# Moving three output groups into the attention's fill, and a final stage that goes token by token

## The chip, the core and the metric

The kernel runs on one core of one Trainium2 chip. The metric is the device time of one launch in microseconds (us). A core has five engines that run their own instruction queues side by side: TensorE (PE; its weight loads are listed as PEld), VectorE (DVE), ScalarE (ACT), GpSimd (POOL) and SyncE (SP). In this kernel SP issues every DMA, in the order of its queue; an issue that waits holds up all that stand behind it.

## The reference

The input is one sequence of 2048 tokens with 1024 values each. One layer is computed: an RMS norm, one input projection to six parts (`q`, `k`, `v`, an attention gate, the input of a recurrence, its gate), two groups of heads, one output projection, an RMS norm and a residual.

```python
h = rmsnorm(x, pre_norm_g)
q, k, v, g_attn, x_lru, g_lru = split(h @ w_in)
o = diff_attention(q, k, v, lam)          # 8 heads, causal, two softmaxes per head, value width 128
y_attn = rmsnorm(o, subln_g) * (1 - lam_init) * silu(g_attn)
y_lru = rg_lru(conv(x_lru)) * silu(g_lru)
y = concatenate([y_attn, y_lru]) @ w_out  # 2048 -> 1024
x = x + rmsnorm(y, post_norm_g)
```

The last norm needs all 1024 outputs of a token, and each output needs all heads. So a token's output can't be finished before the last head's attention on that token is.

## The kernel before, in words

Products of 32-bit values are made of three matmuls: each operand is split into a high part and the rest, and high x high, rest x high and high x rest are added in PSUM. A block of 128 tokens by 512 outputs over 1024 inputs takes 8 x 3 = 24 matmuls of 512 columns; I call it a group.

The program runs in stages: the input projection of the first half of the sequence with the recurrence; attention for tokens 0 to 1023 (with the other half's projection as fill); the second half's recurrence; attention for tokens 1024 to 2047, which matters here; and a final stage.

**The second attention** (`attention`, called with pairs 4 to 7) goes through 8 heads. A pair is 256 tokens, and a head has four pairs of four units (two blocks of 128 tokens, two softmaxes): 128 units, and 12 steps that drain the pipeline. A unit's scores (`s`, L642) are made one step ahead, DVE takes the maximum, ACT the exponentials; some steps later the weights are transposed on PE (`pw`, L715), split by ACT and DVE (`wh`, `wl`, L719 and L720), and multiplied with the values (`o`, L738). Every two pairs of a head (512 tokens, called `j`; `j` = 2 is tokens 1024 to 1535, `j` = 3 the rest) are normalised in six steps: sums over partitions by PE (`pm`, L760), a reciprocal root by DVE (`f`), which goes out to DRAM as `r_s` (L773) and comes back spread over partitions as `rb` (L777), POOL's product `yt` (L782), and the store into `ya_s[j]` (L785). A head's keys come by `ks<-k_s` (L600); the third key block of a head takes the buffer of a block that the head before uses up to its last unit, so it can't be loaded much ahead.

**Fill.** In every step the loop also takes matmuls of the output projection from the generator `fill_out`: 8.25 a step (`FB`). Its groups go through four sets of weights, (rows of `w_out`, half of the outputs): recurrence left and right (16 groups each), attention left and right for the token blocks 0 to 7 (8 each), whose attention part was done in the first half, and one more: attention right for block 8. Sums so far lie in DRAM (`part_s`). In the last set the group is complete on its right, so `finish` (L963) runs the token block's ending: two squares on ACT, two products on POOL, a chain of small DVE operations, an addition to `x`, a store. All groups use one PSUM buffer (`f`), so a group begins when the one before has been read out (L1058). When the set changes, `load_wo` loads eight new blocks of weights through two buffers (`woraw`, L950), each split by POOL. Block `i`'s input is loaded by `load_y` (L958) and split by POOL in quarters (L70, L71).

**Final stage.** Blocks 9 to 15 lack both attention halves, block 8 its left one. The pool `y` holds this stage's tiles. First `load_ya` for blocks 9 and 10; then three right halves (`right`, blocks 9, 10 and 11) with the right weights that are still there, while the eight blocks of left weights come (`woraw`, L1123, two buffers; DVE splits both parts, L203 and L204). Then for each block 8 to 15 its left half and ending (`left`), and after blocks 8 to 11 the right half of the block four further on. `right` loads the partial sums (L1108). The matmuls are `ps_y`, L1098.

The framework keeps each engine's queue in one order that it works out when the program is built, and it makes every wait. What stands in a queue is not always in the order of the source.

Of the kernel before, what the change touches and what calls it, by code (L numbers as in the profile page):

```python
# [18 lines left out]
P = 128  # L19
S = 2048  # L20
D = 1024
# [22 lines left out]
def hymba_kernel(  # L44
# [544 lines left out]

    def attention(prs, kv_p, e_p, a_p, ps_s, ps_w, ps_o, nsb, fill, per_slot, kbufs, vbufs, p1bufs):
        NS = len(prs)
        nmax = (prs[-1] + 1) * 256
# [188 lines left out]

        def norm6(h, j):
            nc.sync.dma_start(out=ya_s[j][:, h, :], in_=nrm.pop((h, j))[1])  # L785

        units = [(h, pr, t, c) for h in range(H) for pr in prs for t in range(2) for c in range(2)]
        U = len(units)
# [43 lines left out]
        for s in range(U + 12):  # L832
            ops = todo.get(s, [])

            def run(kind, fn):
                for k, a in ops:
                    if k == kind:
                        fn(*a)

            for k, fn in (("K", load_k), ("VV", load_v), ("Q", load_q), ("G", load_g)):  # L840
                run(k, fn)
            u = units[s] if s < U else None
            nx = units[s + 1] if s + 1 < U else None
            na = len(pieces(u)[1]) if u else 0
            npc = len(pieces(nx)[1]) if nx else 0
            if u:
                score_exp(u)
            tp = 0.15 + SP / 1200.0
            free = [0.0 if k < nsb - na else tp * (k - nsb + 1 + na) + 0.1 for k in range(npc)]
            ts = [a for k, a in ops if k == "T"]  # L850
            vs = [a + (e,) for k, a in ops if k == "V" for e in range(2)]
            owed += per_slot(s)
            nf = int(owed)
            clock, k = 0.0, 0
            while k < npc or ts or vs or nf > 0:
                if k < npc and (free[k] <= clock or not (vs or ts or nf > 0)):
                    score_mm(nx, k)
                    score_max(nx, k)
                    clock = max(clock, free[k]) + 0.43 * SP / CH
                    k += 1  # L860
                elif ts and clock >= T_AT:
                    transpose_w(*ts.pop(0))
                    clock += 0.43
                elif nf > 0:
                    r = next(fill, "end")
                    if r == "end":
                        nf = 0
                    elif r == "group":
                        owed -= 1
                        nf = 0 if k < npc or s < U else nf  # L870
                    else:
                        nf -= 1
                        owed -= 1
                    clock += 0.216
                elif vs and not ts:
                    values(*vs.pop(0))
                    clock += 0.33
                elif ts:
                    transpose_w(*ts.pop(0))
                    clock += 0.43  # L880
            run("C", combine)
            run("N1", norm1)
            run("N2", norm2)
            run("N3", norm3)
            run("N4", norm4)
            run("N5", norm5)
            run("N6", norm6)
# [123 lines left out]
    with ExitStack() as pb:  # L1011
# [4 lines left out]
        ps_w = pb.enter_context(tc.tile_pool(name="ps_wB", bufs=2, space=PSUM))  # L1016
        ps_o = pb.enter_context(tc.tile_pool(name="ps_oB", bufs=1, space=PSUM))
        ps_f = pb.enter_context(tc.tile_pool(name="ps_fB", bufs=1, space=PSUM))
        groups = [(r, nh, i) for r, nh in wsets for i in range((8, 16)[r])] + [(0, 1, 8)]

        def fill_out():
            ysp, parts = load_y(*groups[0][::2])
# [1 line left out]
                split(*p)  # L1024
            nc.sync.dma_start(out=pgt, in_=post_norm_g[0].partition_broadcast(P))
            for g, (r, nh, i) in enumerate(groups):
                ps = ps_f.tile([P, CH], F32, tag="f", name="f")
                yh, yl = ysp
                nxt = groups[g + 1] if g + 1 < len(groups) else None
                if nxt:  # L1030
                    ysp, parts = load_y(*nxt[::2])
                part = None
                c0 = nh * CH
                if i >= 8 and r == 0:
                    yv = f_p.tile([P, D], F32, tag="yv", name="yv", bufs=1)
                    nc.sync.dma_start(out=yv, in_=part_s[1][i])
                    part = yv[:, CH:]
                    ys[i], yvs[i] = ysp, yv
                elif r == 0:
                    if nh:  # L1040
                        yv = f_p.tile([P, D], F32, tag="yv", name="yv", bufs=1)
                        nc.sync.dma_start(out=yv[:, 0:CH], in_=part_s[0][i][:, 0:CH])
                    part = f_p.tile([P, CH], F32, tag="part", name="part", bufs=1)
                    nc.sync.dma_start(out=part, in_=part_s[1][i][:, c0:c0 + CH])
                for k in range(8):
                    hi, lo = wo[r, nh, k]
                    for m, (a, b) in enumerate(((yh, hi), (yl, hi), (yh, lo))):
                        nc.tensor.matmul(  # L1048
                            out=ps, lhsT=a[:, k, :], rhs=b, start=(k == 0 and m == 0), stop=(k == 7 and m == 2),
                        )  # L1050
                        if (k, m) != (7, 2):
                            yield
                    if nxt and nxt[:2] != (r, nh):
                        load_wo(*nxt[:2], k)
                    if k % 2 and nxt:
                        split(*parts[k // 2])
                if r == 0 and nh == 1:
                    nc.vector.tensor_tensor(out=yv[:, CH:], in0=ps, in1=part, op=ALU.add)  # L1058
                    ends[i] = finish(f_p, i, yv, 1, 1, nc.gpsimd if i < FE else nc.vector)
                    if i < 8:  # L1060
                        ends.pop(i)()
                else:
                    st = f_p.tile([P, CH], F32, tag="fo", name="fo", bufs=1)
                    if part:
                        nc.vector.tensor_tensor(out=st, in0=ps, in1=part, op=ALU.add)
                        nc.sync.dma_start(out=part_s[0][i][:, 0:CH], in_=st)
                    else:
                        nc.scalar.activation(out=st, in_=ps, func=AF.Copy)
                        nc.sync.dma_start(out=part_s[1][i][:, c0:c0 + CH], in_=st)
                yield "group"  # L1070

        attention(
            range(4, 8), kvB_p, e_p, a_p, ps_s, ps_w, ps_o, 4 * CH // SP, fill_out(),
            lambda s: FB if s > 1 else 6, 6, 5, 1,
        )

    with ExitStack() as p3:  # L1080
        y_p = p3.enter_context(tc.tile_pool(name="y", bufs=2))
        ps_y = p3.enter_context(tc.tile_pool(name="ps_y", bufs=6, space=PSUM))

        def load_ya(i):
            raw = y_p.tile([P, 8, P], F32, tag="yraw3", name="yraw3")
            nc.sync.dma_start(out=raw, in_=ya_s[i // 4][:, :, (i % 4) * P:(i % 4 + 1) * P])
            yh = y_p.tile([P, 8, P], F32R, tag="yh3", name="yh3", bufs=6)
            yl = y_p.tile([P, 8, P], F32R, tag="yl3", name="yl3", bufs=6)
            split3(yh, yl, raw, SY)
            ys[i] = (yh, yl)  # L1090

# [11 lines left out]
        w1 = [wo[0, 1, k] for k in range(8)]  # L1103
        w0 = []

        def right(i):
            yvs[i] = y_p.tile([P, D], F32, tag="yv3", name="yv3", bufs=5)
            nc.sync.dma_start(out=yvs[i], in_=part_s[1][i])  # L1108
            ps = out_mm(i, w1)
            nc.vector.tensor_tensor(out=yvs[i][:, CH:], in0=ps, in1=yvs[i][:, CH:], op=ALU.add)  # L1110
            ends[i] = finish(y_p, i, yvs[i], 2, 1 + (i == 15), nc.vector if FY else nc.gpsimd)

        def left(i):
            ps = out_mm(i, w0)
            nc.vector.tensor_tensor(out=yvs[i][:, 0:CH], in0=ps, in1=yvs[i][:, 0:CH], op=ALU.add)
            ends.pop(i)()

        load_ya(9)
        load_ya(10)
        for i in range(9, 12):  # L1120
            for k in ((0, 1, 2), (3, 4, 5), (6, 7))[i - 9]:
                raw = y_p.tile([P, CH], F32, tag="woraw3", name="woraw3")
                nc.sync.dma_start(out=raw, in_=w_out2[k * P:(k + 1) * P, 0:CH])  # L1123
                hi = y_p.tile([P, CH], F32R, name=f"w3h{k}", bufs=1)
                lo = y_p.tile([P, CH], F32R, name=f"w3l{k}", bufs=1)
                split3(hi, lo, raw, SW)
                w0.append((hi, lo))
            right(i)
            load_ya(i + 2)
        for i in range(8, 16):  # L1130
            left(i)
            if i < 12:
                right(i + 4)
                if i + 6 < 16:
                    load_ya(i + 6)
    pf.close()


# [29 lines left out]
```

## Time and profile before

| | |
|---|---|
| median of 3 runs | 2303.52 us (2302.61 to 2305.75) |
| the profiled execution | 2302.22 us |
| its span, first to last instruction | 2300.4 us |
| PE busy | 2183.5 us (95%) |
| DVE, ACT, POOL busy | 64%, 43%, 35% |
| mean granted clock of PE | 0.980 |

A row of the profile names a line of the code, an engine, an operation and its tiles (what it writes, an arrow, what it reads; the numbers of buffers left out). In rows in order of time the first number is the start, counted from the span's start, and the second the length. Matmuls overlap in the pipeline, so a length of 0.39 us does not mean that the next one starts 0.39 later. An entry on SP is the issue of a DMA; its landing is later.

### The profile page before, as it was taken

The page shows a single profiled execution, that of the slowest core. Times are in us where ns is not written, and L with a number is a line of the kernel's source. Part 1 is how long each engine was busy: PE and PEld are TensorE (multiplying, and loading weights), DVE is VectorE, ACT ScalarE, POOL GpSimd, SP SyncE. Part 2 cuts the span into 40 slices and gives each one's busy share as a digit, 9 for nine tenths or more (in the row PEclk, how much of TensorE's full clock was granted, in tenths as well). Part 3 has the DMA queues.
Part 4 walks back from the last instruction along what each step waited for, and adds up shares of the span by engine and source line. Part 5 has one row for each costly group of instructions (what it writes and reads, how often), then busy time and mean ns, then how long its engine had stood idle before and what let it go on. Part 6 is the DMA issues. An engine that isn't in the chain of part 4 may idle for free. (4 is left out here: it accounts for less than half of the span.)

```text
span 2300.4 us, 31837 instructions
## 1 busy us (share of the span) xinstructions
PE 2183.5 (95%) x11281; PEld 1800.9 (78%) x11281; DVE 1482.6 (64%) x2976; ACT 984.2 (43%) x2227; POOL 804.7 (35%) x773
## 2 busy tenths in 40 slices
PE   7999999999899999999989998999999998999778
PEld 6888888888678878888878775888788886887666
DVE  6532145456576666666237786888888887888565
ACT  4311134434443444444125564665555655555211
POOL 1222034444311111111266553233533335345452
PEclk9999999999999999999999998999999999999989
DMA  6554322332569876864452117456466475655473
GB/s 201 155 150 149 112 86 85 105 106 69 141 155 188 169 172 175 183 165 116 128 179 67 60 37 185 105 138 169 112 156 165 111 147 135 173 138 142 113 258 128
DMA packets 358785, 317.94 MB, mean 138 GB/s; under 512 B 32546, under 2 KB 290659, under 8 KB 358627
## 3 DMA queue, kind: packets, MB, share of 16 engines
q1 hardware_dynamic: 358626, 315.91, 52.8%
q8 instruction: 89, 1.46, 0.3%
q14 instruction: 70, 0.57, 0.1%
HBM read 221.41 MB, written 94.44 MB: 137 GB/s over the span
## 5 line engine op out<-in xcount | busy, mean ns | idle before, releaser
L228 PE MATMUL ps<-hh,whi 128*128 128x512 f32 (+1 forms) x1456 | 569.6, 391 | 2.7 <-DVE hilo L245 2.0
L228 PE MATMUL ps<-hh,wlo 128*128 128x512 f32 (+1 forms) x1456 | 567.4, 390 | 0.0
L228 PE MATMUL ps<-hl,whi 128*128 128x512 f32 (+1 forms) x1456 | 565.2, 388 | 1.1 <-DVE hl L446 1.1
L683 ACT ACTIVATE p<-s,nm 128x512 f32<-128x512 f32 (+3 forms) x640 | 392.1, 623 | 328.7 <-DVE nm L667 220.4
L665 DVE TENSOR_REDUCE mx<-s 128x1 f32<-128x512 f32 (+3 forms) x576 | 341.0, 617 | 114.9 <-PE s L642 96.3
L642 PE MATMUL s<-ks,qs 128*128 128x512 f32 (+2 forms) x1280 | 369.7, 387 | 28.9 <-DMA ks<-k_s 16.8
L200 POOL TENSOR_TENSOR wlo<-wraw,whi 128x1024 fp32r<-128x1024 f32 x88 | 222.7, 2531 | 437.3 <-DVE whi L199 133.3
L228 PEld LDWEIGHTS ps<-hh,whi 128*128 128x128 f32 x1456 | 277.6, 191 | 53.6 <-DVE hilo L245 2.4
L228 PEld LDWEIGHTS ps<-hl,whi 128*128 128x128 f32 x1456 | 277.2, 190 | 52.7 <-DVE hl L446 1.4
L228 PEld LDWEIGHTS ps<-hh,wlo 128*128 128x128 f32 x1456 | 276.6, 190 | 51.1
L642 PEld LDWEIGHTS s<-ks,qs 128*128 128x128 f32 x1280 | 216.4, 192 | 82.3 <-ACT p L683 33.0
L719 ACT ACTIVATE wh<-pw 128x512 fp32r<-128x512 f32 (+1 forms) x288 | 160.3, 577 | 186.5 <-PE pw L715 183.0
L738 PE MATMUL o<-wh,vs 128*128 128x256 f32 (+1 forms) x1152 | 222.5, 283 | 0.0
L720 DVE TENSOR_TENSOR wl<-pw,wh 128x512 fp32r<-128x512 f32 (+1 forms) x288 | 185.4, 653 | 35.8 <-ACT wh L719 34.3
L738 PEld LDWEIGHTS o<-wh,vs 128*128 128x128 f32 x1152 | 193.2, 191 | 18.1 <-ACT wh L719 2.1
L70 POOL TENSOR_SCALAR yh<-yraw 128x256 fp32r<-128x256 f32 x196 | 92.3, 488 | 290.6 <-PE f L1048 267.9
L1048 PE MATMUL f<-woh,yh 128*128 128x512 f32 x392 | 163.2, 416 | 25.0 <-DVE yv L1058 17.9
L782 POOL TENSOR_TENSOR yt<-yt,rb 128x512 f32<-128x512 f32 x32 | 44.1, 1379 | 405.4 <-DMA rb<-r_s 218.7
L701 DVE SCALAR_TENSOR_TENSOR p<-p,rr,p 128x128 f32<-128x128 f32 (+15 forms) x128 | 179.2, 1400 | 2.8
L715 PE MATMUL pw<-ident,p 128*128 128x128 f32 x1088 | 169.4, 274 | 5.8 <-DVE wl L720 4.5
L738 PE MATMUL o<-wl,vs 128*128 128x256 f32 x576 | 163.7, 284 | 8.9 <-DVE wl L720 8.9
L1048 PE MATMUL f<-wol,yh 128*128 128x512 f32 x392 | 163.3, 417 | 0.9 <-POOL wol L71 0.9
(166 smaller groups left out, 3298.7 us busy)
## 6 DMA issues: line engine op xcount, KB each, us to landing
wraw<-in_w_in_dram SPq DMA_DIRECT2D x96, 512.0 KB, 4.8
qs<-q_s SPq DMA_DIRECT2D x128, 256.0 KB, 5.2
vs<-v_s SPq DMA_DIRECT2D x48, 512.0 KB, 6.2
ks<-k_s SPq DMA_DIRECT2D x96, 256.0 KB, 5.5
xt<-in_x_dram SPq DMA_DIRECT2D x32, 512.0 KB, 4.7
k_s<-hilo SPq DMA_DIRECT2D x64, 256.0 KB, 4.2
q_s<-hilo SPq DMA_DIRECT2D x64, 256.0 KB, 3.5
v_s<-hilo SPq DMA_DIRECT2D x32, 512.0 KB, 3.7
```

Source lines behind the costliest of these rows:

```text
L70: nc.gpsimd.tensor_scalar(out=hi, in0=src, scalar1=1.0, scalar2=1.0, op0=ALU.mult, op1=ALU.mult)
L200: nc.gpsimd.tensor_tensor(out=lo, in0=src, in1=hi.bitcast(F32), op=ALU.subtract)
L228: nc.tensor.matmul(out=ps[:, t0:t0 + n], lhsT=a[:, k, :], rhs=b[:, k, t0:t0 + n], start=(k == 0 and m == 0), stop=(k == KC - 1 and m == 2),)
L642: nc.tensor.matmul(out=ps[:, b0 - c0:b0 - c0 + nk], lhsT=qq[:, c, t * P:(t + 1) * P], rhs=kst[h, b0 // CH][:, c, 0:nk], start=(m == 0), st ...
L665: nc.vector.tensor_reduce(out=mx[:, pi:pi + 1], in_=sc[u, pi][:, 0:c1 - c0], axis=AX.X, op=ALU.max)
L683: nc.scalar.activation(out=p[:, c0:c1], in_=sc.pop((u, pi))[:, 0:c1 - c0], func=AF.Exp, bias=negm[u], accum_out=acc,)
L701: nc.vector.scalar_tensor_tensor(out=p0[:, 0:n], in0=p1[:, 0:n], scalar=rr[:, 1:2], in1=p0[:, 0:n], op0=ALU.mult, op1=ALU.add,)
L715: nc.tensor.transpose(pw[:, i * P:(i + 1) * P], wts[h, pr, t][:, kb * P:(kb + 1) * P], ident)
L719: nc.scalar.activation(out=wh[:, 0:n], in_=pw[:, 0:n], func=AF.Copy)
L720: nc.vector.tensor_tensor(out=wl[:, 0:n], in0=pw[:, 0:n], in1=wh[:, 0:n].bitcast(F32), op=ALU.subtract,)
L738: nc.tensor.matmul(out=po[h, j][:, oo:oo + w1 - w0], lhsT=a[:, kb % 4, :], rhs=w[:, w0:w1], start=(kb == 0 and m == 0), stop=(kb == 2 * pr ...
L1048: nc.tensor.matmul(out=ps, lhsT=a[:, k, :], rhs=b, start=(k == 0 and m == 0), stop=(k == 7 and m == 2),)
```

## The change

Token blocks are counted 0 to 15. The change does these things:

- The fill's list ends with attention right for blocks 8, 9, 10 and 11, where it had block 8 alone. These four no longer keep their result on the chip: they are added to the partial sums in DRAM (`part_s[1]`, right half) as the left half of blocks 0 to 7 is. The `finish` of block 8 is no longer begun in the fill.
- The fill says "wait" (and the loop leaves it alone for that step) until the last head's store into `ya_s[2]` has been put into the program (`ya_done`). Block 8's input is loaded only then.
- The rate is 9 matmuls a step where it was 8.25. Before, the fill's list ended in the rest behind the loop.
- The final stage loads all eight blocks of left weights first, with ACT making the high part and DVE the rest, then goes through blocks 8 to 15: a left half each, and ahead of it the right half for 12 to 15. Partial sums are loaded two blocks ahead (`begin`). Input of block 8 is loaded again.
- The pool `y` is on the other side of the memory (where attention's pools were), with 5 and 4 buffers in place of 6 and 5.

```diff
+    ya_done = set()
...
         def norm6(h, j):
             nc.sync.dma_start(out=ya_s[j][:, h, :], in_=nrm.pop((h, j))[1])
+            ya_done.add((h, j))
...
+                    elif r == "wait":
+                        nf = 0
...
-        groups = [(r, nh, i) for r, nh in wsets for i in range((8, 16)[r])] + [(0, 1, 8)]
+        groups = [(r, nh, i) for r, nh in wsets for i in range((8, 16)[r])] + [(0, 1, i) for i in range(8, 12)]
...
             for g, (r, nh, i) in enumerate(groups):
+                if ysp is None:
+                    while (H - 1, i // 4) not in ya_done:
+                        yield "wait"
+                    ysp, parts = load_y(r, i)
+                    for p in parts:
+                        split(*p)
...
-                if nxt:
+                ysp, parts = None, ()
+                if nxt and (nxt[0] or nxt[2] < 8 or (H - 1, nxt[2] // 4) in ya_done):
                     ysp, parts = load_y(*nxt[::2])
...
-                if r == 0 and nh == 1:
+                if r == 0 and nh == 1 and i < 8:
                     nc.vector.tensor_tensor(out=yv[:, CH:], in0=ps, in1=part, op=ALU.add)
-                    ends[i] = finish(f_p, i, yv, 1, 1, nc.gpsimd if i < FE else nc.vector)
-                    if i < 8:
-                        ends.pop(i)()
+                    finish(f_p, i, yv, 1, 1, nc.gpsimd)()
...
-                        nc.sync.dma_start(out=part_s[0][i][:, 0:CH], in_=st)
+                        nc.sync.dma_start(
+                            out=part_s[1][i][:, CH:] if i >= 8 else part_s[0][i][:, 0:CH], in_=st,
+                        )
...
-            lambda s: FB if s > 1 else 6, 6, 5, 1,
+            lambda s: 9 if s > 1 else 6, 6, 5, 1,
...
-        y_p = p3.enter_context(tc.tile_pool(name="y", bufs=2))
+        y_p = p3.enter_context(tc.tile_pool(name="y", bufs=2, side="right"))
...
+        def load_w0(k):
+            raw = y_p.tile([P, CH], F32, tag="woraw3", name="woraw3")
+            nc.sync.dma_start(out=raw, in_=w_out2[k * P:(k + 1) * P, 0:CH])
+            hi = y_p.tile([P, CH], F32R, name=f"w3h{k}", bufs=1)
+            lo = y_p.tile([P, CH], F32R, name=f"w3l{k}", bufs=1)
+            nc.scalar.activation(out=hi, in_=raw, func=AF.Copy)
+            nc.vector.tensor_tensor(out=lo, in0=raw, in1=hi.bitcast(F32), op=ALU.subtract)
+            w0.append((hi, lo))
...
-        for i in range(9, 12):
-            for k in ((0, 1, 2), (3, 4, 5), (6, 7))[i - 9]:
...
-            right(i)
-            load_ya(i + 2)
+        for k in range(8):
+            load_w0(k)
+            if k in (3, 6):
+                load_ya(8 + (k > 3))
+        begin(8)
+        begin(9)
         for i in range(8, 16):
+            if i + 2 < 16:
+                load_ya(i + 2)
+                begin(i + 2)
+            if i >= 12:
+                right(i)
             left(i)
-            if i < 12:
-                right(i + 4)
-                if i + 6 < 16:
-                    load_ya(i + 6)
```

What it moves, as the built programs' queues have it. First SP's queue ahead of the load of head 6's third key block (`ks_18181` before, `ks_18335` after); `woraw` are blocks of `w_out`, `part_s` the partial sums. Before:

```order
L950 DMA woraw_18444<-in_w_out_dram 128x512
L950 DMA woraw_18475<-in_w_out_dram 128x512
L950 DMA woraw_18486<-in_w_out_dram 128x512
L950 DMA woraw_18533<-in_w_out_dram 128x512
L950 DMA woraw_20026<-in_w_out_dram 128x512
L1069 DMA part_s1_15_227<-fo_18541 128x512
L950 DMA woraw_20035<-in_w_out_dram 128x512
L623 DMA gt_18729<-g_s6_2_158 128x512
L600 DMA ks_18181<-k_s6_2_118 64x1024 x2
```

After:

```order
L618 DMA qs_18531<-q_s6_2_86 64x4x256 x2
L1071 DMA part_s0_1_205<-fo_18484 128x512
L1051 DMA part_18545<-part_s1_2_214 128x512
L963 DMA yraw_18929<-ya_s1_197 128x8x128
L1071 DMA part_s0_2_206<-fo_18667 128x512
L1051 DMA part_18691<-part_s1_3_215 128x512
L602 DMA ks_18335<-k_s6_2_118 64x1024 x2
```

The reloads of `w_out` came directly ahead of the keys; now they come 14 rows or more earlier, and a partial-sum store stands there.

Second, SP's queue at the end of attention, from the last head's `r_s` for `j` = 3 on (`ya_s_199` is `ya_s[3]`, `ya_s_198` is `ya_s[2]`). Before:

```order
L773 DMA r_s_3_195<-f_21374 128x4x1
L777 DMA rb<-r_s_3_195 128x512
L986 DMA out_dram<-xt 128x1024
L1042 DMA yv<-part_s_6_210 128x512
L1044 DMA part<-part_s_7_219 128x512
L785 DMA ya_s_199<-yt 128x512
L977 DMA xt<-in_x_dram 128x1024
L1086 DMA yraw_21548<-ya_s_198 128x8x128
L1086 DMA yraw_21554<-ya_s_198 128x8x128
L986 DMA out_dram<-xt 128x1024
L1042 DMA yv<-part_s_7_211 128x512
L1123 DMA woraw_21560<-in_w_out_dram 128x512
```

After:

```order
L775 DMA r_s_3_195<-f_21587 128x4x1
L779 DMA rb<-r_s_3_195 128x512
L1071 DMA part_s_10_222<-fo 128x512
L1051 DMA part<-part_s_11_223 128x512
L787 DMA ya_s_199<-yt 128x512
L1115 DMA woraw_21672<-in_w_out_dram 128x512
L1071 DMA part_s_11_223<-fo 128x512
L1115 DMA woraw_21678<-in_w_out_dram 128x512
L1093 DMA yraw_21696<-ya_s_198 128x8x128
L1115 DMA woraw_21684<-in_w_out_dram 128x512
L1093 DMA yraw_21720<-ya_s_198 128x8x128
L1115 DMA woraw_21690<-in_w_out_dram 128x512
```

In both the final stage's loads stand behind that store; now the left weights are the first of them.

Third, PE's queue where the final stage begins (`f` is the fill, `ps_y` the final stage, `woh`/`wol` the right weights already there, `w3h`/`w3l` the left ones). Before:

```order
L1048 MATMUL f<-woh_20205,yl 128x512
L1048 MATMUL f<-wol_20206,yh 128x512
L1098 MATMUL ps_y<-woh_20028,yh_21550 128x512
L1098 MATMUL ps_y<-woh_20028,yl_21551 128x512
L1098 MATMUL ps_y<-wol_20029,yh_21550 128x512
```

After:

```order
L1055 MATMUL f<-woh_19666,yl 128x512
L1055 MATMUL f<-wol_19667,yh 128x512
L1105 MATMUL ps_y<-w3h_21674,yh_21698 128x512
L1105 MATMUL ps_y<-w3h_21674,yl_21699 128x512
L1105 MATMUL ps_y<-w3l_21675,yh_21698 128x512
```

Three right halves with weights at hand stood first; now the first matmul needs a left block.

More of the change, by code (lines that the diff above doesn't have):

```diff
@@ L1033, in fill_out @@
                 c0 = nh * CH
[L1034 to L1040, printed above, removed]
+                if r == 0:
+                    if nh and i < 8:
                         yv = f_p.tile([P, D], F32, tag="yv", name="yv", bufs=1)
@@ L1054, in fill_out @@
                         load_wo(*nxt[:2], k)
-                    if k % 2 and nxt:
+                    if k % 2 and parts:
                         split(*parts[k // 2])
-                if r == 0 and nh == 1:
+                if r == 0 and nh == 1 and i < 8:
                     nc.vector.tensor_tensor(out=yv[:, CH:], in0=ps, in1=part, op=ALU.add)
-                    ends[i] = finish(f_p, i, yv, 1, 1, nc.gpsimd if i < FE else nc.vector)
-                    if i < 8:
-                        ends.pop(i)()
+                    finish(f_p, i, yv, 1, 1, nc.gpsimd)()
                 else:
@@ L1086, in load_ya @@
             nc.sync.dma_start(out=raw, in_=ya_s[i // 4][:, :, (i % 4) * P:(i % 4 + 1) * P])
-            yh = y_p.tile([P, 8, P], F32R, tag="yh3", name="yh3", bufs=6)
-            yl = y_p.tile([P, 8, P], F32R, tag="yl3", name="yl3", bufs=6)
+            yh = y_p.tile([P, 8, P], F32R, tag="yh3", name="yh3", bufs=5)
+            yl = y_p.tile([P, 8, P], F32R, tag="yl3", name="yl3", bufs=5)
             split3(yh, yl, raw, SY)
@@ L1104, in hymba_kernel, with begin @@
         w0 = []
+        def load_w0(k):
[6 more added lines that the diff above has]
+            w0.append((hi, lo))
+        def begin(i):
+            yvs[i] = y_p.tile([P, D], F32, tag="yv3", name="yv3", bufs=4)
+            nc.sync.dma_start(out=yvs[i], in_=part_s[1][i])
         def right(i):
-            yvs[i] = y_p.tile([P, D], F32, tag="yv3", name="yv3", bufs=5)
-            nc.sync.dma_start(out=yvs[i], in_=part_s[1][i])
             ps = out_mm(i, w1)
             nc.vector.tensor_tensor(out=yvs[i][:, CH:], in0=ps, in1=yvs[i][:, CH:], op=ALU.add)
-            ends[i] = finish(y_p, i, yvs[i], 2, 1 + (i == 15), nc.vector if FY else nc.gpsimd)
         def left(i):
+            ends[i] = finish(y_p, i, yvs[i], 2, 1 + (i == 15), nc.gpsimd)
             ps = out_mm(i, w0)
@@ L1116, in left @@
             ends.pop(i)()
-        load_ya(9)
-        load_ya(10)
-        for i in range(9, 12):
-            for k in ((0, 1, 2), (3, 4, 5), (6, 7))[i - 9]:
[L1122 to L1127, printed above, removed]
-            right(i)
-            load_ya(i + 2)
-        for i in range(8, 16):
+        for k in range(8):
[4 more added lines that the diff above has]
+        begin(9)
+        for i in range(8, 16):
+            if i + 2 < 16:
[3 more added lines that the diff above has]
+                right(i)
             left(i)
-            if i < 12:
-                right(i + 4)
-                if i + 6 < 16:
-                    load_ya(i + 6)
     pf.close()
```

## The prediction

> **What bounds the kernel now.** I read the page first, then busy time by stretch, then TensorE (PE) in order of time around its waits, then the DMA queue of SyncE (SP) around the same places.
>
> ```profile
> span 2300.4 us, 31837 instructions
> PE 2183.5 (95%) x11281; PEld 1800.9 (78%) x11281; DVE 1482.6 (64%) x2976; ACT 984.2 (43%) x2227; POOL 804.7 (35%) x773
> ```
>
> PE is busy for 95% of the span and the change leaves its matmuls as they are, so only PE's idle time (some 117 us) can be won or lost. By stretch (length, then busy time of PE, PEld, DVE, ACT, POOL):
>
> ```profile
> 1480.00:1573.00 93.00, 90.65 (x545) 75.62 (x544) 76.85 (x167) 56.32 (x152) 31.00 (x45) 1.00 0.62 134
> 2033.00:2124.40 91.40, 86.08 (x489) 70.08 (x490) 78.01 (x171) 50.65 (x142) 49.97 (x64) 0.98 0.55 147
> 2124.40:2165.70 41.30, 33.02 (x192) 28.07 (x190) 26.22 (x62) 11.74 (x28) 14.85 (x21) 0.92 0.53 116
> 2165.70:2203.00 37.30, 21.61 (x81) 17.04 (x82) 22.56 (x44) 4.34 (x12) 23.18 (x25) 0.77 0.59 188
> ```
>
> An ordinary head (first row) leaves 2.4 us idle in 93; the two stretches at the end of attention lose 8.3 and 15.7. Here is PE at the waits (start, length, and in brackets the idle time before it and what ended it):
>
> ```profile
> 1566.44 0.47 PE L642 MATMUL s<-ks,qs 128*128 128x256 f32 x2 [1.51 <-DMA ks<-k_s]
> 1940.45 0.77 PE L642 MATMUL s<-ks,qs 128*128 128x256 f32 x2 [10.04 <-DMA ks<-k_s]
> 2124.43 0.72 PE L760 MATMUL pm<-ones,sq 128*128 128x2 f32 x6
> 2165.66 1.05 PE L760 MATMUL pm<-ones,sq 128*128 128x2 f32 x8
> 2167.72 0.47 PE L1048 MATMUL f<-woh,yh 128*128 128x512 f32 x1 [1.00 <-DVE f L766]
> 2195.42 0.77 PE L1048 MATMUL f<-woh,yh 128*128 128x512 f32 x1 [12.20 <-DVE yv L1058]
> 2195.99 0.63 PE L1048 MATMUL f<-woh,yl 128*128 128x512 f32 x1
> 2196.42 0.63 PE L1048 MATMUL f<-wol,yh 128*128 128x512 f32 x1
> 2291.30 0.40 PE L1098 MATMUL ps_y<-w3h,yl 128*128 128x512 f32 x1
> 2291.53 0.40 PE L1098 MATMUL ps_y<-w3l,yh 128*128 128x512 f32 x1
> ```
>
> A warm 512-column matmul takes 0.23 us (last two rows); after a long wait they come every 0.43, and nine did so after 2195.42, which is 1.8 us more. The two `pm` rows are my marks: M1 (2124.43) begins the normalisation of head 7's rows 1024 to 1535, M2 (2165.66) that of its rows 1536 to 2047. PE's last matmul ends at 2291.93, 167.5 us after M1; the final 8.4 us are the last token's ending, which the change leaves alone. And SP's queue:
>
> ```profile
> 1916.35 14.76 SPq L950 DMA_DIRECT2D woraw<-in_w_out_dram  x6
> 1934.12 1.11 SPq L600 DMA_DIRECT2D ks<-k_s  x2
> 2137.45 0.37 SPq L773 DMA_DIRECT2D r_s<-f  x1
> 2147.85 0.33 SPq L777 DMA_DIRECT2D rb<-r_s  x1
> 2154.90 0.32 SPq L785 DMA_DIRECT2D ya_s<-yt  x1
> 2173.56 0.37 SPq L773 DMA_DIRECT2D r_s<-f  x1
> 2181.38 0.32 SPq L777 DMA_DIRECT2D rb<-r_s  x1
> 2188.32 0.32 SPq L785 DMA_DIRECT2D ya_s<-yt  x1
> 2190.78 1.24 SPq L1086 DMA_DIRECT2D yraw<-ya_s  x2
> 2195.39 1.32 SPq L1123 DMA_DIRECT2D woraw<-in_w_out_dram  x2
> ```
>
> From M1 to the store of `ya_s` it took 13.0 to `r_s`, 10.4 to `rb`, 7.1 to `ya_s`: 30.5 us. From M2: 7.9, 7.8 and 6.9, so 22.7, and 2.5 more to the first load of the final stage, which the program makes wait for that store. SP issues in order, so whatever stands behind `rb` waits for `r_s` too.
>
> **The change part by part.**
>
> *Denser fill, 9 matmuls a unit for 8.25.* It moves work, no cost of its own: by the program's order 133 fill matmuls and 360 of the final stage follow M1 before, 111 and 288 after. So 94 go ahead of M1, which comes 94 x 0.23 = 21.6 us later. It also moves the reloads of `w_out`. In before, eight `woraw` issues, each waiting for POOL's splitting, stand right ahead of head 6's `ks`, and PE waits 10.04 where an ordinary head waits 1.51. In after, some 17 us of PE work or more lie between any such reload and the next head's `ks`. I take 8.5 us off, and the 1.8 of cold matmuls: **-10** (bounds -12 and 0, the latter if the partial-sum store that now stands there is late).
>
> *Endings earlier.* Three of the eight groups with a full ending (`finish`) lie before M1 now, seven after. The stretch up to M1 idles 5.3 us against 2.4 with three of them, so four more could cost 4; DVE is busy 78 of 91 us there against 77 of 93, hardly more. I take **+2** (0 to +8, if DVE fills up).
>
> *Rows 8 to 11 as fill.* Their first matmul needs `ya_s` of M1's chain back from DRAM. The pieces:
>
> ```profile
> yraw<-ya_s SPq DMA_DIRECT2D x11, 512.0 KB, 4.5
> woraw<-in_w_out_dram SPq DMA_DIRECT2D x8, 256.0 KB, 3.7
> L71 POOL TENSOR_TENSOR yl<-yraw,yh x22: 718/734/751, 2100.3 to 2190.7; 128x256 fp32r<-128x256 f32 x22
> L70 POOL TENSOR_SCALAR yh<-yraw x21: 395/405/1369, 2099.9 to 2190.2; 128x256 fp32r<-128x256 f32 x21
> L719 ACT ACTIVATE wh<-pw 128x512 fp32r<-128x512 f32 x38 | 21.9, 602 | 35.0 <-PE pw L715 34.7
> L204 DVE TENSOR_TENSOR w3l<-woraw,w3h x8: 676/693/2775, 2202.7 to 2226.1; 128x512 fp32r<-128x512 f32 x8
> 2148.14 1.03 PE L715 MATMUL pw<-ident,p 128*128 128x128 f32 x8
> 2127.34 0.94 PE o L738 x8
> ```
>
> Chain: `r_s` issued M1 + 11 (between 13.0 and 7.9), `rb` 9.1 later, `ya_s` 7.0, its landing 2.5, the load 4.5, POOL's first quarter 0.4 + 0.7: M1 + 35.3. PE has until then 0.8 of `pm`, 15 fill matmuls (3.5), 42 transposes (5.4) and 68 value matmuls (8.0): 17.7. So PE waits about 17.6 us. Before, other fill covered this chain. Bounds: 28 (`r_s` and `rb` as quick as in M2's chain, less work on DVE) to 41 (M1's 30.5, and the rest).
>
> From there to M2: 24 matmuls, nine cold (7.3), 8 value matmuls that stand behind the first of them (0.9), two changes of group of 1.0 each (the row of 2167.72: one PSUM buffer, so DVE's addition lies between), 24 matmuls (5.5), 9 (2.1): 17.8. The added partial-sum loads and stores, 256 KB each, lie beside these and I cost them at nothing.
>
> *The final stage without cover.* Before, three right halves, whose weights were already there, ran while the eight blocks of the left weights came. Now the first token needs those blocks at once, and their loads stand behind M2's `r_s`, `rb` and `ya_s` on SP. `r_s` M2 + 7 (7.9 before, when DVE had a token's ending beside it), then 7.8, 6.9 and 2.5: first `woraw` at M2 + 24.2. Two buffers: a round is the landing 3.7, ACT's copy 0.6, DVE's subtraction 0.7 and the issue 0.35, 5.4 us. The second block is issued 0.8 after the first, the eighth three rounds later, at 17.0; it is split at 22.0 and its three matmuls end at 22.7. So token 8's left half ends at M2 + 46.9, where PE's own work (15 fill matmuls left in this group, 24 in the next, 24 here, `pm`) is 15.5. Bounds 37 (rival 1 below) and 55 (M1's 30.5 for the 21.7 to the store).
>
> Then 264 matmuls remain: 60.7, and 1.8 for nine cold ones. The pool on the other side reuses memory of finished attention tiles; the first load waits for M2's `ya_s` store either way, so nothing there.
>
> **Sum.** M1 to the last matmul: 35.3 + 17.8 + 46.9 + 60.7 + 1.8 = 162.5. With 21.6 for the later M1 that is 184.1 against 167.5: **+16.6**. With -10 and +2: **+8.6 us**. The profiled execution took 2302.22 (span 2300.4 and 1.8 around it), so 2310.8; the median of the runs is 1.3 higher, 2303.52, which makes **2312**.
>
> **A rule against the change.** The slowest `w3l` subtraction ran beside POOL:
>
> ```profile
> 2219.94 2.58 POOL L204 TENSOR_TENSOR yl<-yraw,yh 128x1024 fp32r<-128x1024 f32 x1
> 2220.30 2.77 DVE L204 TENSOR_TENSOR w3l<-woraw,w3h 128x512 fp32r<-128x512 f32 x1
> ```
>
> DVE's 0.7 us operation ended 0.5 after POOL's, at 2.77. In the stretch above POOL makes three such `yl` operations (tokens 8, 9, 10), and each can meet one `w3l`; two in the same buffer's rounds cost 2 x 2.1 = 4.2 us. That is a rival below. The Trainium skill (SBUF — State Buffer, section "SBUF: two separate sides") says that VectorE, in an operation with two SBUF inputs, and GpSimd lock one pair of ports against each other for a whole instruction; by that rule every meeting costs the rest of POOL's operation, and the sum would be 2316. The two rows agree with it.
>
> **The rivals.** Two more views bear on them (waits of PE: total, times, longest; landing times, least, median and most, of `r_s` and then of the final stage's `woraw`):
>
> ```profile
> PE s L642 <- ACT p L683: 8.3, 6, 2.5
> PE pw L715 <- DVE wl L720: 4.5, 4, 1.9
> DMA to landing us min/median/max: 3.5/6.9/11.0
> DMA to landing us min/median/max: 2.5/3.7/5.2
> ```
>
> 1. *Faster: the round trips through DRAM are quick when little else is in flight.* M1's chain as fast as M2's was (7.9, 7.8, 6.9): 30.4, that is 4.9 less. In M2's chain `r_s` at 5 for 7 and `rb` 4.0 later for 7.8 (the least landing is 3.5): 5.8 less; `woraw` at its least, 2.5 for 3.7, in three rounds and the last landing: 4.8 less. Sum -15.5: 2296.5. It decides when the drained attention leaves the queues empty; against it, M2's chain in before ran in the same emptiness and took 22.7. The Trainium skill (DMA: Bandwidth & Descriptors, "Anatomy of one DMA — SWDGE (gpsimd) path") fits 2 us plus bytes over 436 GB/s per DMA, some 2 us for the 2 KB of `r_s` and 2.6 for a `woraw`; by that estimate the time would be about 2296. The rows (7.8 to `rb`, 3.7) speak against it for `r_s`.
> 2. *No change: denser fill also covers PE's small waits.* PE waited 8.3 us for ACT's exponentials and 4.5 for the split weights. If two thirds go, 8 us are won in addition: 2304.
> 3. *Slower still: DVE is the bound.* The port lock above (4.2) and seven endings before M1 that cost 8 and not 2: 2312 + 10 = 2322.
> 4. *The change does not do what it says:* by the order, rows 8 to 11 stand behind all transposes and nearly all value matmuls, so they hardly fill anything. This is in the forecast already.
>
> **Chances.** Forecast 0.44, rival 1 0.18, rival 2 0.18, rival 3 0.20. The forecast's own range is 2303 to 2321: its bounds lie up to 10 away in the tail and at head 6, and don't all fall on one side. The range reaches from rival 1, 2296, to just over rival 3, 2325. A measurement of this kernel tells about 0.2% (4.6 us) from no change: slower 0.62 (rival 3 and nearly all of the forecast), same 0.20, faster 0.18.
>
> **What would show it.** Right: no wait of 10 us for `ks` at head 6; one of 12 to 23 us ahead of the first of rows 8 to 11, ended by POOL's `yh`; a wait of over 12 us ahead of the first final matmul and several of 1 to 3 inside token 8; the last matmuls without waits. Wrong: final weights issued before M2's `ya_s`, a first wait under 8 us, or M1 no later than about 2136 - or above 2146, with waits for DVE in head 7.

## The result, and the profile after

The changed kernel takes 2322.01 us (median of 6 runs, 2317.87 to 2328.68), the kernel before 2303.49 (6 runs on the same chip): a ratio of 1.0089, interval 1.0076 to 1.0102, so 18.5 us slower. The profiled execution is one of the longer ones, 2326.41; the second attention also begins 3.6 later in it than in the profile before (first fill matmul at 1395.59, not 1391.97), ahead of anything that the change touches.

```profile
span 2324.6 us, 31897 instructions
PE 2192.1 (94%) x11281; PEld 1808.4 (78%) x11281; DVE 1462.6 (63%) x2967; ACT 989.6 (43%) x2235; POOL 820.3 (35%) x800
```

PE in order of time, at the marks and the longer waits, as the prediction showed it for before:

```profile
1575.75 0.47 PE L644 MATMUL s<-ks,qs 128*128 128x256 f32 x2 [2.20 <-DMA ks<-k_s]
1656.55 0.50 PE L1055 MATMUL f<-woh,yh 128*128 128x512 f32 x1 [2.02 <-POOL woh L70]
2043.21 0.50 PE L1055 MATMUL f<-woh,yh 128*128 128x512 f32 x1 [2.19 <-POOL woh L70]
2136.01 0.87 PE L717 MATMUL pw<-ident,p 128*128 128x128 f32 x3 [5.93 <-DVE wl L722]
2161.33 0.84 PE L762 MATMUL pm<-ones,sq 128*128 128x2 f32 x7
2191.22 0.79 PE L1055 MATMUL f<-woh,yh 128*128 128x512 f32 x1 [5.08 <-POOL yh L70]
2208.60 0.61 PE L762 MATMUL pm<-ones,sq 128*128 128x2 f32 x5
2236.95 0.77 PE L1105 MATMUL ps_y<-w3h,yh 128*128 128x512 f32 x1 [17.32 <-DMA woraw<-in_w_out_dram]
2239.57 0.79 PE L1105 MATMUL ps_y<-w3h,yl 128*128 128x512 f32 x1 [1.85 <-POOL yl L204]
2315.79 0.39 PE L1105 MATMUL ps_y<-w3l,yh 128*128 128x512 f32 x1
```

The reader is to see two things. M1 has moved from 2124.43 to 2161.33, by 36.9, where 94 more fill matmuls account for 21.6 and the stages ahead for 3.6; so 11.7 has been lost between the start of attention and M1. And from M1 to the last matmul it is 154.9, where it was 167.5 with those 94 in it: 9.0 of new idle time behind M1.

To find the 11.7 I cut the stage at every `pm`, which gives half heads. In the changed kernel each full one holds the same 72 fill matmuls. Changed kernel (from, to, length, then busy PE, PEld, DVE, ACT, POOL, granted clock, DMA share, GB/s):

```profile
1618.36:1669.69 51.33, 47.05 (x267) 37.65 (x265) 38.88 (x81) 27.78 (x77) 31.67 (x41) 1.00 0.42 120
1718.40:1764.41 46.01, 45.73 (x267) 37.88 (x266) 37.32 (x80) 27.61 (x76) 16.13 (x25) 1.00 0.33 88
1906.15:1958.05 51.90, 48.98 (x267) 39.79 (x266) 42.64 (x81) 25.85 (x73) 24.48 (x36) 0.93 0.56 147
1958.05:2003.61 45.56, 45.45 (x282) 39.04 (x281) 36.88 (x82) 25.41 (x69) 14.72 (x25) 1.00 0.81 181
2003.61:2056.76 53.15, 48.91 (x266) 38.82 (x265) 39.94 (x87) 27.01 (x77) 33.84 (x42) 0.97 0.44 126
2056.76:2106.74 49.98, 46.70 (x281) 39.05 (x281) 45.63 (x113) 27.98 (x77) 25.36 (x32) 1.00 0.90 218
2106.74:2161.33 54.59, 48.20 (x266) 40.03 (x265) 45.12 (x119) 30.75 (x87) 22.39 (x25) 0.94 0.56 120
```

Before, the half head with the change of weights ahead of the second set, an ordinary one, head 6's, and the last one:

```profile
1650.50:1699.41 48.91, 46.03 (x276) 38.90 (x275) 39.35 (x77) 25.95 (x71) 23.04 (x33) 0.97 0.90 205
1699.41:1744.85 45.44, 45.07 (x260) 36.64 (x259) 38.77 (x80) 28.22 (x77) 19.38 (x25) 1.00 0.27 77
1926.15:1980.40 54.25, 44.20 (x271) 38.20 (x270) 37.63 (x80) 24.17 (x65) 21.86 (x34) 0.91 0.79 191
2071.21:2124.43 53.22, 48.13 (x260) 38.03 (x259) 45.63 (x107) 30.61 (x87) 30.80 (x41) 0.97 0.57 154
```

Head 6's half head fell from 54.25, with 61 fill matmuls, to 45.56 with 72: 8.7 shorter with 2.5 more work, so 11.2 won, as forecast. But the three half heads in which the weights change (51.33, 51.90, 53.15) are 18.3 longer together than three ordinary ones of the same half of a head (46.0), where before one of 48.91 lost 3.5. That is the place that the prediction did not price. The last two before M1, with the endings, grew too, by some 4 beyond what they lost before. Some 3 more lie ahead of the first mark (82.4 from the stage's first fill matmul to the first `pm`, for 77.5 before, of which eight more fill matmuls are 1.8); no run takes these apart. Together that is about the 11.7.

One of the waits in the last half head, followed upstream (DVE and POOL in order of time):

```profile
2128.29 1.30 POOL L784 TENSOR_TENSOR yt<-yt,rb 128x512 f32<-128x512 f32 x1 [8.61 <-DMA rb<-r_s]
2129.55 2.48 POOL L978 TENSOR_TENSOR yv<-yv,pgt 128x512 f32<-128x512 f32 x2
2132.06 1.41 DVE L988 SCALAR_TENSOR_TENSOR xt<-yv,ss,xt 128x1024 f32<-128x1024 f32 x1 [7.18 <-POOL yv L978]
```

A fill ending's last operation on DVE (`xt`) waits for a product on POOL, which stands in POOL's queue behind `yt`, which waits for `rb` from DRAM. DVE stands for 7.18 us, and attention's own `wl` behind it keeps PE for the 5.93 shown above.

### The profile page after: what moved, and what is told of

Its sections match the earlier page's. It is cut to its first block, busy times and chain, and to the rows that moved or that the text cites. A ratio compares the mean times of both kernels' runs of the same rounds, so it can differ in the third digit from the quotient of the medians.

```text
span 2324.6 us, 31897 instructions
## 1 busy us (share of the span) xinstructions
PE 2192.1 (94%) x11281; PEld 1808.4 (78%) x11281; DVE 1462.6 (63%) x2967; ACT 989.6 (43%) x2235; POOL 820.3 (35%) x800
## 5 line engine op out<-in xcount | busy, mean ns | idle before, releaser
L1055 PE MATMUL f<-woh,yh 128*128 128x512 f32 x416 | 170.4, 410 | 18.1 <-POOL yh L70 5.8
L717 PE MATMUL pw<-ident,p 128*128 128x128 f32 x1088 | 173.5, 277 | 11.9 <-DVE wl L722 10.3
L1055 PE MATMUL f<-wol,yh 128*128 128x512 f32 x416 | 172.5, 415 | 3.0 <-POOL wol L71 2.9
L1055 PE MATMUL f<-woh,yl 128*128 128x512 f32 x416 | 170.2, 409 | 0.1
```

Source lines behind the costliest of these rows:

```text
L717: nc.tensor.transpose(pw[:, i * P:(i + 1) * P], wts[h, pr, t][:, kb * P:(kb + 1) * P], ident)
L1055: nc.tensor.matmul(out=ps, lhsT=a[:, k, :], rhs=b, start=(k == 0 and m == 0), stop=(k == 7 and m == 2),)
```

## The experiments

My theory after the trace: the rate does all the harm, in attention at the reloads of weights and at the endings, and behind M1 because fewer fill matmuls are left there; the new final stage costs nothing. The rivals: the final stage costs it (the forecast's view), or engines that are simply full. All ratios are to the kernel before on the same chip:

| kernel | median us | ratio and interval |
|---|---|---|
| e1 before, rate 9 | 2325.15 | 1.0102 (1.0085 to 1.0120) |
| e2 changed, rate 8.25 | 2298.03 | 0.9991 (0.9979 to 1.0002) |
| e3 before, four reload buffers | 2298.20 | 0.9983 (0.9972 to 0.9995) |
| e4 changed, four reload buffers | 2318.62 | 1.0071 (1.0051 to 1.0092) |
| e5 changed, ending products on DVE | 2333.42 | 1.0119 (1.0100 to 1.0139) |
| e6 changed, reload split by ACT and DVE | 2338.86 | 1.0149 (1.0130 to 1.0167) |
| e7 changed, both | 2340.77 | 1.0168 (1.0149 to 1.0187) |
| e8 e6 at rate 8.25 | 2311.30 | 1.0034 (1.0018 to 1.0050) |
| e9 changed, `rb` and `ya_s` issued by POOL | 2380.08 | 1.0342 (1.0318 to 1.0365) |
| e10 before, the same | 2348.05 | 1.0200 (1.0179 to 1.0221) |
| e11 e9 at rate 8.25 | 2345.26 | 1.0186 (1.0170 to 1.0201) |
| e12 e4 at rate 8.25 | 2295.31 | 0.9965 (0.9951 to 0.9979) |

### The two halves of the change apart (e1, e2)

e1 is the kernel before with the gate on block 8's input and the new rate:

```diff
-            lambda s: FB if s > 1 else 6, 6, 5, 1,
+            lambda s: 9 if s > 1 else 6, 6, 5, 1,
```

> The kernel before with the denser fill alone (9 matmuls a unit, and block 8's input loaded only once its rows are stored); the final stage is before's. Theory: the denser fill itself costs the attention stage time, so M1 (first sum of the last head's rows 1024 to 1535) comes at 2155 to 2162 as in the changed kernel, the 10-us wait for head 6's keys is gone, and with 94 fewer fill matmuls behind M1 the tail waits as the changed kernel's does: 2315 to 2322 in all. Rival A (the forecast: denser fill wins 8, only the new final stage costs): M1 at 2138, 2300 to 2306. Rival B (the rate does nothing to the sum, the final stage is all): 2303 within 4.

e2 is the changed kernel with that line put back:

> The changed kernel with the old rate of 8.25: new final stage, rows 8 to 11 as fill. Theory: M1 at 2124 with head 6's 10-us wait as before; 205 fill matmuls follow M1, so the first normalisation is covered and no wait stands ahead of row 8; what is left is the wait behind M2's chain: 2293 to 2303, not slower than before. Rival A (the forecast's tail term, final stage without cover): some 2312. Rival B (the final stage is all): 2318 to 2322.

The rate alone gives 1.0102, the whole change 1.0089 (the intervals overlap), the new final stage alone 0.9991 (its interval takes in 1). e1's time lies 3 above its theory's range, e2's inside it. So the slowdown is the rate, and the forecast's view of the final stage falls. The gate on block 8's input is in both kernels, so it is not what parts them. e1's M1, M2 and first final matmul:

```profile
2157.63 0.61 PE L762 MATMUL pm<-ones,sq 128*128 128x2 f32 x5
2201.01 1.05 PE L762 MATMUL pm<-ones,sq 128*128 128x2 f32 x8 [0.73 <-ACT sq L752]
2225.73 0.76 PE L1110 MATMUL ps_y<-woh,yh 128*128 128x512 f32 x1 [23.66 <-DVE yh L203]
```

And e2's head 6, M2 and its longest wait behind the final stage's start:

```profile
1943.40 0.77 PE L644 MATMUL s<-ks,qs 128*128 128x256 f32 x2 [10.25 <-DMA ks<-k_s]
2166.92 0.85 PE L762 MATMUL pm<-ones,sq 128*128 128x2 f32 x4
2215.35 0.50 PE L1105 MATMUL ps_y<-w3h,yl 128*128 128x512 f32 x1 [1.50 <-POOL yl L204]
```

The wait ahead of the first final matmul is 23.66 with the old final stage and no fill behind M2 (e1), 17.32 with the new one and 39 fill matmuls, and gone with the new one and 144 (e2). The three right halves of the old stage are no cover there: their inputs are loaded behind M2's store as well. Fill is the cover, and the rate decides how much is left.

### More buffers for the reload (e3, e4)

Two of four raw buffers lie in a small pool of their own:

```diff
-        raw = f_p.tile([P, CH], F32, tag="woraw", name="woraw", bufs=2)
+        raw = wr[k % 4 // 2].tile([P, CH], F32, tag="woraw", name="woraw", bufs=2)
```

> The kernel before with four buffers for the reloaded weights in place of two, two of them in a small pool of their own. Theory: head 6's keys were late because the reloads stood in SP's queue waiting for a buffer; with four they go out earlier, the 10-us wait shrinks to under 4, and the time to 2293 to 2297. Rival: POOL's splits set the pace of the reload (8 blocks of 2.2 us each), the wait stays at 8 or more and the time at 2303.

> The changed kernel with four buffers for the reloaded weights. Theory: the waits for POOL's woh and wol at the three changes of weights (0.5 to 2.2 us each, and cold matmuls behind them) come from the two buffers: 3 to 8 us less, 2314 to 2319. Rival: POOL itself is too slow for 9 matmuls a unit (2.2 us a block against 1.9 us of matmuls a block): the waits stay, 2322.

e3: the rival was the better one for the wait (7.3 left of 10.0). The total of waits, and SP's issues:

```profile
PE s L642 <- DMA ks<-k_s: 7.3, 1, 7.3
```

```profile
1917.66 12.12 SPq L951 DMA_DIRECT2D woraw<-in_w_out_dram  x6
```

Six issues in 12.12 us are 2.0 each, the pace of POOL's splits (0.62 + 1.29 a block). e4: the half heads with a change of weights fall to 48.07, 47.47 and 47.85, 13.0 less than in the changed kernel; so there it was the two buffers. But the next half head takes half of it back:

```profile
1613.88:1661.95 48.07, 45.77 (x266) 37.88 (x265) 38.60 (x81) 27.64 (x77) 32.56 (x41) 1.00 0.45 128
1900.26:1947.73 47.47, 46.33 (x267) 37.71 (x266) 40.32 (x81) 25.85 (x73) 21.93 (x35) 1.00 0.58 153
1993.85:2041.70 47.85, 46.92 (x267) 37.71 (x265) 39.31 (x87) 27.01 (x77) 31.35 (x40) 1.00 0.45 120
2041.70:2098.68 56.98, 49.56 (x282) 41.41 (x281) 47.07 (x112) 28.09 (x77) 27.84 (x34) 0.94 0.83 200
```

```profile
2069.09 1.28 DVE L989 SCALAR_TENSOR_TENSOR xt<-yv,ss,xt 128x1024 f32<-128x1024 f32 x1 [3.44 <-DMA xt<-in_x_dram]
```

56.98 for 49.98: the endings' loads now meet attention at another phase, and DVE stands 3.44 for one. The median is 3.4 under the changed kernel's, though the intervals of the two ratios overlap.

### Taking POOL out of it (e5 to e8)

```diff
-                    finish(f_p, i, yv, 1, 1, nc.gpsimd)()
+                    finish(f_p, i, yv, 1, 1, nc.vector)()
```

> The changed kernel (rate 9), the two products of each fill ending (blocks 0 to 7) on DVE and not on POOL. Theory: in the changed kernel DVE once stands 7.18 us for such a product, which stands in POOL's queue behind yt, which waits for rb from DRAM; PE then waits 5.93 for DVE's wl. With the products on DVE that wait goes, at 16 x 0.7 us of DVE work: 2313 to 2318. Rival: DVE is simply full in heads 6 and 7, and more work on it costs more: 2322 to 2330.

```diff
-        split(hi, lo, raw)
+        nc.scalar.activation(out=hi, in_=raw, func=AF.Copy)
+        nc.vector.tensor_tensor(out=lo, in0=raw, in1=hi.bitcast(F32), op=ALU.subtract)
```

(for the three later sets of weights)

> The changed kernel (rate 9), the reloaded weights split by ACT (high part) and DVE (rest) and not by POOL. Theory: PE loses 7 to 9 us in each of the three half heads in which the weights change, against 2 elsewhere, because POOL, in order behind yt, begins the splits late and makes a block every 1.95 us; without POOL these go to 2 to 4: 2308 to 2314. Rival: the two buffers and the landing (3.7 us) set the pace whoever splits: 2319 to 2323.

> The changed kernel with both edits (reload split by ACT and DVE, ending products on DVE). Theory: the denser fill's loss in the attention stage is POOL's queue in these two places, so M1 falls from 2161 to 2140 to 2148, and the time to 2301 to 2308; what remains above that of the old rate is the thinner cover behind M1. Rival: DVE, with 11 + 17 us more work, becomes the bound: no better than the better one of the two alone.

> The changed kernel at the old rate of 8.25 with the reload split by ACT and DVE. Theory: the 10-us wait for head 6's keys is reloads that stand in SP's queue for POOL's splits; without POOL it goes to under 3 us: 2286 to 2292, faster than both kernels. Rival: the keys wait for the buffers' round trip all the same: 2296 to 2300.

All four have a higher ratio than what they were made from (e5's interval just touches the changed kernel's): the theory that taking POOL out wins the time falls. The rivals named a full DVE or the buffers' round trip. e6 shows something sharper than either, in PE, DVE, ACT and SP at one change of weights:

```profile
1643.51 1.65 PE L644 MATMUL s<-ks,qs 128*128 128x512 f32 x4 [7.86 <-ACT p L685]
1642.82 0.69 DVE L962 TENSOR_TENSOR wol<-woraw,woh 128x512 fp32r<-128x512 f32 x1 [7.12 <-ACT woh L961]
1642.16 0.63 ACT L961 ACTIVATE woh<-woraw 128x512 fp32r<-128x512 f32 x1 [8.08 <-DMA woraw<-in_w_out_dram]
1631.40 0.32 SPq L779 DMA_DIRECT2D rb<-r_s  x1
1638.09 0.33 SPq L787 DMA_DIRECT2D ya_s<-yt  x1
1638.52 0.86 SPq L955 DMA_DIRECT2D woraw<-in_w_out_dram  x2
```

DVE is idle for 7.12 us, not full. ACT's copy waits for a block whose load SP issued only behind `ya_s`, and attention's exponentials stand behind that copy. In e5 ACT stands in the same way for another load behind `ya_s`, at an ending's square, which the edit does not move; in the changed kernel such a square waited 0.9 at most for its load. ACT in order of time:

```profile
2088.16 0.63 ACT L977 ACTIVATE junk<-yv 128x512 f32<-128x512 f32 x1 [7.15 <-DMA yv<-part_s]
```

So, as far as these rows show it, the time is lost where an engine that attention needs holds, in its queue, work on data whose load is late. On POOL such work waited at less cost in these runs; on ACT and DVE it stopped attention. How much of e5 and e6 is that and how much the added DVE work itself, these runs do not part.

### Taking the normalisation out of SP's queue (e9 to e11)

```diff
-            nc.sync.dma_start(out=rb, in_=r_s[h][j].partition_broadcast(P))
+            nc.gpsimd.dma_start(out=rb, in_=r_s[h][j].partition_broadcast(P))
-            nc.sync.dma_start(out=ya_s[j][:, h, :], in_=nrm.pop((h, j))[1])
+            nc.gpsimd.dma_start(out=ya_s[j][:, h, :], in_=nrm.pop((h, j))[1])
```

> The changed kernel (rate 9), with two DMAs of each normalisation, the load of rb and the store of ya_s, issued by POOL and not by SP; POOL waits for rb in any case. Theory: what loses time is SP's queue, which stands behind rb for the round trip of r_s (7 to 10 us) with reloads, keys, partial sums and the final stage's loads behind it. Freed, the half heads with a change of weights lose 3 to 5 instead of 7 to 9, and the final left weights are issued before M2's ya_s, so the 17.3-us wait ahead of the first final matmul falls under 8: 2295 to 2308. Rival A: POOL's queue, which still stands for rb, is the limit: the attention stage stays, only the tail gains: 2308 to 2316. Rival B: the final loads wait for memory that attention still holds, or POOL's own issues cost as much: 2318 to 2325.

> The kernel before, with rb and ya_s issued by POOL. Theory: its final loads (inputs of blocks 9 and 10, left weights) no longer stand behind M2's ya_s, and the tail loses some 10 less of its 25; head 6's wait for keys stays at 7 to 10, since those reloads wait for POOL's splits: 2290 to 2296. Rival: nothing moves, the tail is bound by M2's chain itself: 2300 to 2304.

> The changed kernel at the old rate of 8.25, with rb and ya_s issued by POOL. Theory: as in the other two, the tail behind M2 loses 10 less (it loses 21 with SP issuing), 2285 to 2292, and the new final stage, weights first, gains more from it than the old one. Rival: 2296 to 2300, as with SP issuing.

All three missed by far: 45 to 58 us slower than with SP. The edit reaches the first attention too, so that e9's first mark of the second attention already comes at 1496.60 for 1477.97. What the runs do settle is the tail. e9 behind M2 (2255.76):

```profile
2258.97 0.37 SPq L775 DMA_DIRECT2D r_s<-f  x1
2270.56 0.59 POOL L779 DMA_DIRECT2D rb<-r_s  x1 [13.40 <-DMA r_s<-f]
2275.66 0.59 POOL L787 DMA_DIRECT2D ya_s<-yt  x1 [0.30 <-POOL yt L784]
2278.21 0.33 SPq L1115 DMA_DIRECT2D woraw<-in_w_out_dram  x1
2285.34 0.77 PE L1105 MATMUL ps_y<-w3h,yh 128*128 128x512 f32 x1 [18.52 <-DMA woraw<-in_w_out_dram]
```

SP has nothing of the normalisation left ahead of `woraw` but `r_s`, and still issues it 2.55 after `ya_s`: as in the changed kernel, 2.05. So it is not the queue: the load waits for the store itself, whose tile holds memory that the pool `y` takes over (rival B, and what the prediction had said). And POOL, which now stands for `r_s` as well as `rb` (13.40 here), is late with everything else. That a block's loads could come earlier with memory released earlier was not tried.

### What is left as a version (e12)

> What is left of all this as a version: the new final stage at the old rate of 8.25, with four buffers for the reloaded weights. Each of the two alone came out some 3 us under the kernel before. Theory: they act in different places (head 6's wait for keys, and the stretch behind M2), so they add: 2292 to 2297, head 6's wait at 7 and not 10, tail behind M2 losing 21 and not 25. Rival: both were within what a measurement tells from nothing, and so is their sum: 2298 to 2303.

2295.31, a ratio of 0.9965 (0.9951 to 0.9979): faster than both kernels, if by 0.35% only against the one before. Head 6's wait is 7.9, and from M2 (2162.97) to the last matmul (2284.88) it is 121.9 where before had 126:

```profile
1938.71 0.55 PE L644 MATMUL s<-ks,qs 128*128 128x256 f32 x1 [7.92 <-DMA ks<-k_s]
2162.97 1.05 PE L762 MATMUL pm<-ones,sq 128*128 128x2 f32 x8
2284.88 0.39 PE L1107 MATMUL ps_y<-w3l,yh 128*128 128x512 f32 x1
```

The time lies in the theory's range and the profile has both gains in their places. That they add is likely, but not shown by the times alone: e2's interval takes in 1, and e12's overlaps e3's. Rates between 8.25 and 9 were not tried.

## Why the prediction was right in sign and range, and wrong in its sum

It gave 2312 (2296 to 2325); it is 2322.0. The sign is right, but not for the reason given: the forecast let the attention win 8 and the stretch behind M1 lose 16.6, and they lost 11.7 and 9.0, both by the rate (e1, e2). Against the profiled execution it lacked 15.6 us: 23.3 too early at M1 (3.6 of it run variation in earlier stages), and 7.6 too many behind M1. That the two have opposite signs is luck: without the second one the time would lie above the range.

- **Head 6's keys, -10:** right, -11.2.
- **"It moves work, no cost of its own":** this is the step that failed. The denser fill costs some 18 in the three half heads that change weights, where before lost 3.5 in one and head 6's wait in another. At 9 matmuls a unit the three of a block are used in 1.9 us (45.8 us a half head, 8 units), while with two buffers POOL began to split the last four blocks of the second set at 1648.77, 1651.81, 1655.87 and 1659.96, one in 3.7; e4 shows that the buffers were the reason (13.0 back with four, though 7.0 were lost again in the half head behind). The prediction saw the reloads move away from head 6's keys and did not ask whether they can keep up where they now stand.
- **Endings earlier, +2 (0 to +8):** some +4, but not because DVE fills up. DVE stands, 7.18 us at one place, for an ending's product behind `yt` on POOL. That is the sign which the prediction named against itself: M1 above 2146 with a wait for DVE in head 7. The cause of the 4 is read from the trace; no run shows it alone, and e5, which took the product off POOL, was slower.
- **M1 to row 8, 35.3:** 29.9. The wait was 5.08 there and some 4 in smaller ones ahead, not 17.6: `r_s` went out at M1 + 9.2 and not 11, `rb` 9.1 later as forecast, `ya_s` 4.8 behind that and not 7.0, and the cold or waiting transposes filled more of it.
- **Row 8 to M2, 17.8:** 17.4.
- **Token 8's left half, 46.9 (37 to 55):** 46.8; DVE takes up its result at 2255.43. The parts differ. The first left weights were issued at M2 + 20.4, not 24.2: `r_s` was out at M2 + 3.2, not 7, since no ending stood beside it on DVE, and `ya_s` at 18.4, not 21.7. From the first to the eighth issue it took 18.7, not 17.0 (the port lock, below), and 7.7 more to the last matmul, not 5.7. The wait ahead of the first final matmul came as said (17.32, over 12), and e9 bears out that the first load waits for `ya_s`. But the missing right halves were not its reason: e1, with the old order, waits longer. It is the rate that took the cover.
- **The rest, 62.5:** 60.8, by two errors that nearly cancel. The forecast let PE do nothing for other tokens until token 8 was through, but PE's queue mixes the tokens: 52 of the 288 final matmuls, not 24, had ended by 2255.43, which is 6.4 less work behind it. And there are two waits for POOL's `yl` behind it (1.94 and 2.33), where the forecast had none, and more matmuls at the slow pace.
- **Rivals.** 1 (quick round trips) was right for M1's chain, 5.4 less than forecast where it said 4.9; behind M2 it was not: the store was 3.3 sooner, but the weights behind it took that back, and token 8's left half came 0.1 sooner. 2 (denser fill covers small waits) did not show: the waits for ACT's exponentials went from 8.3 to 7.6, those for `wl` from 4.5 to 10.3. 3 gave the time (2322), by another road than a full DVE: seven endings cost some 4, not 8, its port lock 1.8, not 4.2, and the reloads, which it did not have, the most. 4 held: rows 8 to 11 stand behind nearly everything, and e2 shows that the new final stage alone is worth nothing that can be told from noise, and no loss.

The port lock of the prediction's rule did come, on PE's path. POOL and DVE in the changed kernel's final stage (the last row takes up token 8's left half):

```profile
2240.74 2.37 POOL L204 TENSOR_TENSOR yl<-yraw,yh 128x1024 fp32r<-128x1024 f32 x1 [1.23 <-DVE yh L203]
2241.18 2.49 DVE L1119 TENSOR_TENSOR w3l<-woraw,w3h 128x512 fp32r<-128x512 f32 x1 [0.52 <-ACT w3h L1118]
2255.43 1.29 DVE L1133 TENSOR_TENSOR yv<-ps_y,yv 128x512 f32<-128x512 f32 x2 [2.03 <-PE ps_y L1105]
```

Four of the eight `w3l` ran beside an operation of POOL and took 1.19 to 2.49 for 0.69, each ending some 0.55 after POOL's. The one shown, of the fourth block, held the buffer of the sixth, whose load SP issued at 2243.70; the other three on the way to the eighth block ran alone, so the lock cost that chain 1.8. An ending's `xt` on DVE, 1.28 us alone, took 2.07 and 2.30 beside POOL. All this agrees with the Trainium skill (SBUF — State Buffer, "SBUF: two separate sides").

## What to carry to other kernels

A fill's rate is not free: it sets how fast its operands are used up, where its own endings meet the host loop, and how much cover is left for the last round trips; price each reload as buffers against use, at the place where it will stand. When an engine is idle behind a late load, moving that work to a faster engine moves the wait to it; put it on the engine whose standing still hurts least, or bring the load forward. And where a load seems to stand behind another in a queue, ask first whether it waits for memory.

## What the runs showed of the hardware

The store of `r_s`, 2 KB written as single 4-byte values, took a median of 8.4 us from issue to landing in the changed kernel, longer than the 3.4 of a `woraw` of 256 KB. The fit of the Trainium skill (DMA: Bandwidth & Descriptors, "Anatomy of one DMA — SWDGE (gpsimd) path"), which the prediction's first rival used, would give it some 2 us by size as an estimate. But that fit is for DMAs that GpSimd issues, and SP issues this one; for it the runs show some four times as much, and no run here times `r_s` issued by POOL. An issue of `rb` or `ya_s` occupied POOL for 0.59 (e9), SP for 0.32 (the changed kernel).
